# Interleaving two fp32 tensors: every tile DMA split into two, for the even and the odd partitions

## The chip, the core and the metric

The kernel runs on one core of a Trainium2 chip. The metric is the device time of one execution in microseconds (us); lower is better. Before the change the median of three runs was 314.24 us (314.24 to 314.25).

## What is computed

Two fp32 tensors of 32 x 256 x 1024 are interleaved element by element into one of twice the length. Nothing is calculated; every byte is read once, moved to its new place and written once.

```python
def reference(x, y):
    batch, seq, dim = x.shape          # 32, 256, 1024
    result = np.zeros((batch, seq, dim * 2), dtype=np.float32)
    result[..., 0::2] = x
    result[..., 1::2] = y
    return result
```

x and y are 33.55 MB each and the output is 67.11 MB, so 134.22 MB cross between HBM (the chip's large memory) and SBUF (the core's working memory, 128 partitions wide).

## The kernel before

Each tensor is taken as one flat run of elements and cut into n = 8 tiles of 128 x 8192 fp32 (4 MB). Partition p of a tile holds row p, a run of 8192 elements (32 KB) that lies in one piece in HBM. The output of one x tile and one y tile is 128 rows of 16384 elements; it is made and stored in two halves of 128 x 8192, called h = 0 and h = 1.

SBUF holds two tiles of x (`xt`), two of y (`yt`) and two output halves (`ot[0]` for h = 0, `ot[1]` for h = 1). Tile k uses `xt[k % 2]` and `yt[k % 2]`.

Three engines work, each with its own list of instructions, tied by semaphores:

- SyncE (SP) issues the loads. The first half of x's tile 0 is loaded at line 45, then y's tile 0 (line 55), and from there x's tile k (line 52) and y's tile k (line 55) in turn. From tile 2 on, SP waits before each load until VectorE has read the buffer for the last time: `woven` at 4(k-2)+3 for x (line 50) and 4(k-2)+4 for y (line 54).
- VectorE (DVE) does the interleaving with 32 copies of 128 x 4096 elements: for each half, line 67 writes the x elements to the even columns of `ot[h]` and line 70 the y elements to the odd ones. It waits for the loads (`xsem`, `ysem`, and `hsem` for the second half of x's tile 0) and for the stores of the same half of the tile before (`osem[h]`, line 66), whose buffer it overwrites. Each copy adds 1 to `woven`.
- ScalarE (ACT) issues the stores (line 76), one for each half as soon as both its copies are done; the very first half is stored in two parts, of 2048 and 6144 columns. It also loads the second half of x's tile 0 (line 46).

Each DMA adds 16 to its semaphore when it has ended, so the waits count in steps of 16; `stored(k, h)` at line 42 works out how many stores of half h came before tile k. In the profile, SP's DMAs run on queue q1 and ACT's on q10; both queues feed the same 16 DMA engines. After the kernel is built, `tile_interleave_kernel` moves the first DMA of SP and the first of ACT (lines 45 and 46) ahead of the program's opening barrier. At the end ACT and SP wait for the last stores and set the semaphores back.

In the order of the work only the semaphores matter: SP runs ahead up to two tiles, ACT follows VectorE, and VectorE needs a loaded tile and an output half whose last store has ended.

Of the kernel before, what the change touches and what calls it, by code (L numbers as in the profile page):

```python
# [3 lines left out]


def _interleave(nc, x, y, out):
    P = 128
    W = 8192
    H = W // 2  # L10

    total = 1
    for s in x.shape:
        total *= s
    n = total // (P * W)
    assert n * P * W == total

    def rows(ap, names, k):
        flat = ap.rearrange("b s d -> (b s d)")
        return flat[k * names : (k + 1) * names].rearrange("(p w) -> p w", p=P)  # L20

    fp32 = mybir.dt.float32
    xt = [nc.alloc_sbuf_tensor(f"xt{b}", [P, W], fp32).ap() for b in (0, 1)]
    yt = [nc.alloc_sbuf_tensor(f"yt{b}", [P, W], fp32).ap() for b in (0, 1)]
    ot = [nc.alloc_sbuf_tensor(f"ot{b}", [P, W], fp32).ap() for b in (0, 1)]

    xsem = [nc.alloc_semaphore(f"xsem{b}") for b in (0, 1)]
    hsem = nc.alloc_semaphore("hsem")
    ysem = [nc.alloc_semaphore(f"ysem{b}") for b in (0, 1)]
    woven = nc.alloc_semaphore("woven")  # L30
    osem = [nc.alloc_semaphore(f"osem{b}") for b in (0, 1)]

    xs = [rows(x, P * W, k) for k in range(n)]
    ys = [rows(y, P * W, k) for k in range(n)]
    os_ = [rows(out, 2 * P * W, k) for k in range(n)]

    Q = W // 4

    def parts(k, h):
        return [slice(0, W)] if k or h else [slice(0, Q), slice(Q, W)]  # L40

    def stored(k, h):
        return 16 * sum(len(parts(j, h)) for j in range(k))

    nc.sync.dma_start(out=xt[0][:, :H], in_=xs[0][:, :H]).then_inc(xsem[0], 16)
    nc.scalar.dma_start(out=xt[0][:, H:], in_=xs[0][:, H:]).then_inc(hsem, 16)
    for k in range(n):
        b = k % 2
        if k >= 2:
            nc.sync.wait_ge(woven, 4 * (k - 2) + 3)  # L50
        if k:
            nc.sync.dma_start(out=xt[b], in_=xs[k]).then_inc(xsem[b], 16)
        if k >= 2:
            nc.sync.wait_ge(woven, 4 * (k - 2) + 4)
        nc.sync.dma_start(out=yt[b], in_=ys[k]).then_inc(ysem[b], 16)

    for k in range(n):
        b = k % 2
        for h in (0, 1):
            c = slice(h * H, (h + 1) * H)  # L60
            if h == 0:
                nc.vector.wait_ge(xsem[b], 16 * (k // 2 + 1))
            elif k == 0:
                nc.vector.wait_ge(hsem, 16)
            if k:
                nc.vector.wait_ge(osem[h], stored(k, h))
            nc.vector.tensor_copy(out=ot[h][:, 0::2], in_=xt[b][:, c]).then_inc(woven, 1)  # L67
            if h == 0:
                nc.vector.wait_ge(ysem[b], 16 * (k // 2 + 1))
            nc.vector.tensor_copy(out=ot[h][:, 1::2], in_=yt[b][:, c]).then_inc(woven, 1)  # L70

    for k in range(n):
        for h in (0, 1):
            nc.scalar.wait_ge(woven, 4 * k + 2 * h + 2)
            for c in parts(k, h):
                nc.scalar.dma_start(
                    out=os_[k][:, h * W : (h + 1) * W][:, c], in_=ot[h][:, c]
                ).then_inc(osem[h], 16)

    nc.scalar.wait_ge(osem[0], stored(n, 0))  # L80
    used = sorted(s.num for s in [*xsem, hsem, *ysem, woven, osem[0]])
    assert used == list(range(used[0], used[-1] + 1)), used
    nc.scalar.sem_clear(range(used[0], used[-1] + 1))
    nc.sync.nop(nofuse=True).wait_op(osem[1], stored(n, 1), "sem-ge").then_inc(
        osem[1], -stored(n, 1)
    )


def kernel(tc, x, y, out):
    nc = tc.nc  # L90
    tc.close()
    tc.compile()

    _interleave(nc, x, y, out)

    blocks = nc.main_func.blocks
    for engine in (mybir.EngineType.SP, mybir.EngineType.Activation):
        opening = blocks[0].instructions
        at, moved = next(
            (b, i)  # L100
            for b in blocks[1:]
            for i in b.instructions
            if i.engine == engine and i.opcode == "DMACopy"
        )
        assert not (moved.sync_info and moved.sync_info.on_wait)
        body = at.instructions
        body.remove(moved)
        gate = next(
            n
            for n, i in enumerate(opening)  # L110
            if i.engine == engine and i.opcode == "Drain"
        )
        opening.insert(gate, moved)
        at.instructions = body
        blocks[0].instructions = opening


# [1 line left out]
_INS = ['x', 'y']  # L119
_OUTS = [((32, 256, 2048), 'float32')]  # L120


# [23 lines left out]
```

## Time and profile before

| | |
|---|---|
| median of 3 runs | 314.24 us |
| profiled execution | 314.21 us |
| its span, first to last instruction | 312.9 us |
| HBM read / written | 67.11 MB / 67.11 MB, 429 GB/s over the span |
| VectorE x copies, L67 | 16, mean 2295 ns |
| VectorE y copies, L70 | 16, mean 2288 ns |
| VectorE idle before L67 for a store to end | 206.3 us in 14 waits, longest 28.9 |
| a store of 4096 KB, issue to landing (median) | 34.1 us |
| a y load of 4096 KB, issue to landing (median) | 41.5 us |
| an x load of 4096 KB, issue to landing (median) | 24.4 us |

The span is what the profile covers; the execution has 1.3 us more around it. A DMA here is one instruction that moves a whole tile; the 16 DMA engines share its rows, and what the profile calls a packet is one row's transfer on one engine. "Share of 16 engines" is the summed time of the packets over sixteen times the span. The time from issue to landing of a DMA includes what it waits for behind others on the same engines. "L67" is line 67 of the kernel.

### The profile page before, as it was taken

Reading aid. Unit: us, or ns where it says so; the run is one execution under the profiler, and the core shown is the slowest. Engines: PE = TensorE matmul, PEld = TensorE weight load, DVE = VectorE, ACT = ScalarE, POOL = GpSimd, SP = SyncE. Lnnn points to the kernel's source line nnn. Section 1 sums busy time; section 2 is a strip of 40 time slices with the busy share of each in tenths; the row PEclk is TensorE's granted clock in tenths of the full one; section 3 lists DMA queues with packets and bytes.
Section 4 is the critical chain, followed back from the end, with each engine's and each line's share of the span. In section 5 each row is a group of like instructions: output and inputs, shape, how many; then the busy total and the mean of one; then the engine's idle time right before and its main releaser. Section 6 shows DMA issues by size and latency. Waiting matters only on the chain.

```text
span 312.9 us, 114 instructions
## 1 busy us (share of the span) xinstructions
DVE 71.9 (23%) x32; POOL 0.2 (0%) x4
## 2 busy tenths in 40 slices
DVE  0216000501305023050230503205032050415400
POOL 0000000000000000000000000000000000000000
DMA  8999999999999999999999999999999999999998
GB/s 344 461 406 431 436 402 431 440 465 406 448 423 431 440 406 465 402 469 402 469 402 465 406 457 415 436 436 419 452 402 469 402 469 402 469 402 461 411 444 360
DMA packets 4896, 134.22 MB, mean 429 GB/s; under 512 B 544, under 2 KB 544, under 8 KB 544
## 3 DMA queue, kind: packets, MB, share of 16 engines
q10 hardware_dynamic: 2592, 69.21, 51.3%
q1 hardware_dynamic: 2304, 65.01, 48.5%
HBM read 67.11 MB, written 67.11 MB: 429 GB/s over the span
## 4 chain that ended last, share of the span: by engine, by line
DMA 82%; DVE 12%; issue 0%
DMA out_dram<-ot 76%; DMA yt<-in_y_dram 7%; DVE ot L70 6%; DVE ot L67 6%
## 5 line engine op out<-in xcount | busy, mean ns | idle before, releaser
L67 DVE COPY ot<-xt 128x4096 f32<-128x4096 f32 x16 | 36.7, 2295 | 218.0 <-DMA out_dram<-ot 206.3
L70 DVE COPY ot<-yt 128x4096 f32<-128x4096 f32 x16 | 36.6, 2288 | 8.0 <-DMA yt<-in_y_dram 8.0
L130 POOL MEMSET const-uint8-127<- 128x1 uint8 x1 | 0.1, 102 | 0.0
L130 POOL MEMSET const-bfloat16-1.0<- 128x1 bf16 x1 | 0.1, 101 | 0.0
L130 POOL MEMSET const-float32-0.0<- 128x1 f32 x1 | 0.1, 98 | 0.2 <-issue 0.2
L130 POOL MEMSET const-float32-1.0<- 128x1 f32 x1 | 0.1, 98 | 0.0
## 6 DMA issues: line engine op xcount, KB each, us to landing
out_dram<-ot ACTq DMA_DIRECT2D x15, 4096.0 KB, 34.1
yt<-in_y_dram SPq DMA_DIRECT2D x8, 4096.0 KB, 41.5
xt<-in_x_dram SPq DMA_DIRECT2D x7, 4096.0 KB, 24.4
out_dram<-ot ACTq DMA_DIRECT2D x1, 3072.0 KB, 32.8
xt<-in_x_dram SPq DMA_DIRECT2D x1, 2048.0 KB, 11.7
xt<-in_x_dram ACTq DMA_DIRECT2D x1, 2048.0 KB, 13.4
out_dram<-ot ACTq DMA_DIRECT2D x1, 1024.0 KB, 16.1
```

Source lines behind the costliest of these rows:

```text
L67: nc.vector.tensor_copy(out=ot[h][:, 0::2], in_=xt[b][:, c]).then_inc(woven, 1)
L70: nc.vector.tensor_copy(out=ot[h][:, 1::2], in_=yt[b][:, c]).then_inc(woven, 1)
L130: nc = _bacc.Bacc("TRN2", target_bir_lowering=False, num_devices=1)
```

## The change

Partition 2i+r of a tile, with i from 0 to 63 and r 0 or 1, now holds row 64r+i in place of row 2i+r. As one DMA can't walk the partitions in that order, a helper `move` issues two: r = 0 moves rows 0 to 63 into or out of partitions 0, 2, ... 126, and r = 1 moves rows 64 to 127 into or out of partitions 1, 3, ... 127. Each adds 16 to the semaphore, so all counts of DMA semaphores double. All loads and stores go through `move`; x, y and the output halves are permuted alike, and VectorE's copies stay what they were. Two DMAs in place of one are moved ahead of the opening barrier on SP and on ACT.

```diff
+    R = 2
+
     def rows(ap, names, k):
+
         flat = ap.rearrange("b s d -> (b s d)")
-        return flat[k * names : (k + 1) * names].rearrange("(p w) -> p w", p=P)
+        return flat[k * names : (k + 1) * names].rearrange("(r i w) -> r i w", r=R, i=P // R)
+
+    def move(eng, sem, out, in_, c=slice(None), d=None):
+
+        d = c if d is None else d
+        for r in range(R):
+            to = out[r, :, d] if len(out.shape) == 3 else out[r::R, d]
+            of = in_[r, :, c] if len(in_.shape) == 3 else in_[r::R, c]
+            eng.dma_start(out=to, in_=of).then_inc(sem, 16)
...
     def stored(k, h):
-        return 16 * sum(len(parts(j, h)) for j in range(k))
+        return 16 * R * sum(len(parts(j, h)) for j in range(k))
 
-    nc.sync.dma_start(out=xt[0][:, :H], in_=xs[0][:, :H]).then_inc(xsem[0], 16)
-    nc.scalar.dma_start(out=xt[0][:, H:], in_=xs[0][:, H:]).then_inc(hsem, 16)
+    move(nc.sync, xsem[0], xt[0], xs[0], slice(0, H))
+    move(nc.scalar, hsem, xt[0], xs[0], slice(H, W))
...
-            nc.sync.dma_start(out=xt[b], in_=xs[k]).then_inc(xsem[b], 16)
+            move(nc.sync, xsem[b], xt[b], xs[k])
...
-        nc.sync.dma_start(out=yt[b], in_=ys[k]).then_inc(ysem[b], 16)
+        move(nc.sync, ysem[b], yt[b], ys[k])
...
-                nc.vector.wait_ge(xsem[b], 16 * (k // 2 + 1))
+                nc.vector.wait_ge(xsem[b], 16 * R * (k // 2 + 1))
...
-                nc.scalar.dma_start(
-                    out=os_[k][:, h * W : (h + 1) * W][:, c], in_=ot[h][:, c]
-                ).then_inc(osem[h], 16)
+                to = slice(h * W + c.start, h * W + c.stop)
+                move(nc.scalar, osem[h], os_[k], ot[h], c, to)
...
-    for engine in (mybir.EngineType.SP, mybir.EngineType.Activation):
+    for engine, count in ((mybir.EngineType.SP, 2), (mybir.EngineType.Activation, 2)):
+        for _ in range(count):
```

## The prediction, made before the changed kernel ran

> **What bounds the kernel now.** I read the page from its head: engines, then the DMA queues, then the chain, then the DMA issues.
>
> ```profile
> span 312.9 us, 114 instructions
> ## 1 busy us (share of the span) xinstructions
> DVE 71.9 (23%) x32; POOL 0.2 (0%) x4
> ...
> DMA packets 4896, 134.22 MB, mean 429 GB/s; under 512 B 544, under 2 KB 544, under 8 KB 544
> ## 3 DMA queue, kind: packets, MB, share of 16 engines
> q10 hardware_dynamic: 2592, 69.21, 51.3%
> q1 hardware_dynamic: 2304, 65.01, 48.5%
> ```
>
> The only computing engine works 23% of the time. The two DMA queues (q1 is SP's, q10 ACT's) together fill 51.3 + 48.5 = 99.8% of sixteen DMA engines. The packets count themselves: 34 DMAs of 128 rows are 4352, and 34 x 16 = 544 small ones carry the semaphore increments. So one row of a tile is one packet, each DMA gives each engine eight rows, and each engine ends its share with one small packet.
>
> ```profile
> DMA 82%; DVE 12%; issue 0%
> DMA out_dram<-ot 76%; DMA yt<-in_y_dram 7%; DVE ot L70 6%; DVE ot L67 6%
> ```
>
> The chain is DMA, with VectorE as its link. A chain step that is DVE is no idle time of the DMA engines: the busy time by stretches shows that they work through it.
>
> ```profile
> core 0: us, DVE busy (x) POOL busy (x), PEclk, DMA share, GB/s
> 0.00:12.00 12.00, 0.30 (x1) 0.20 (x4) 1.00 0.98 393
> 12.00:24.00 12.00, 3.98 (x2) 0.00 (x0) 1.00 1.00 431
> 24.00:58.00 34.00, 5.12 (x4) 0.00 (x0) 1.00 0.99 418
> 58.00:270.00 212.00, 49.06 (x22) 0.00 (x0) 1.00 1.01 434
> 270.00:303.00 33.00, 13.49 (x6) 0.00 (x0) 1.00 1.01 434
> 303.00:312.80 9.80, 0.00 (x0) 0.00 (x0) 1.00 0.87 374
> ```
>
> The reader is to see that the DMA share is full from 12 us to 303 us, whether loads alone run (431 GB/s at 12 to 24 us) or loads and stores (434). So the limit is one for each DMA engine, not for a direction. The trace's packet records give its size: 3777 of the 3840 packets of 32 KB took 1213 ns exactly, loads and stores alike. An engine's bytes, 134.22 MB / 16 / 32 KB = 256 such packets, need 256 x 1.213 = 310.5 us. That leaves 2.4 us of the span for the head (the first packet starts at 1.0 us, and the first 16 KB packets take 0.9 to 1.6 us each, later ones 0.61) and the tail. The profiled execution took 314.21 us, 1.3 more than its span; the median of the three runs is 314.24. What follows is counted from 314.21.
>
> One more thing lies in the packet records. The sixteen engines go in step: about 60.5 us all sixteen start a packet of q10 within 0.33 us, 1.21 us later all start one of q1, and the last round at 311 us still starts within 0.33 us. So at nearly every moment all engines move rows in one direction, and at the same place of their share.
>
> **The change, part by part.**
>
> Instructions. SP issues 32 DMAs for 16, ACT 36 for 18; VectorE's 32 copies are the same, on the same 128 partitions.
>
> ```profile
> 79.16 0.33 SPq L52 DMA_DIRECT2D xt<-in_x_dram  x1
> 81.36 0.33 SPq L55 DMA_DIRECT2D yt<-in_y_dram  x1
> ```
>
> An issue takes 0.33 us (0.33 to 0.48). The second x issue of a pair ends at about 79.8, and the next wait on SP opens at 81.36: 1.5 us of slack, nothing is late. On ACT the second store follows its first by about 0.34 us; the first gives each engine four rows, 4 x 1.213 = 4.9 us of work, so no engine runs dry. If an engine did, each of the 17 stores would cost up to 0.34 us, 5.8 us in all: that is the price without this cover, and I count 0. In the head the second x issue delays the opening barrier, and so y's first issue (1.57 us), by about 0.4 us; the first x tile gives the engines work until 11.7 us. Cost 0.
>
> Semaphore packets. Each engine gets 34 more, of 9 ns each (6 ns from start to the next packet's start): 0.2 to 0.3 us on the path that sets the end. No gap follows one today: the next packet starts at its end. I take 0.3. The waits on VectorE ask for twice the count and open when the second half has landed, which by bytes is the same moment: 0.
>
> Rows by engine. This is the part that decides. The bytes of one engine are unchanged if all sixteen take four rows of each half. But which rows lie side by side is new: a DMA now steps over every second partition. No row of the trace shows how 64 rows two partitions apart are dealt out, so I bound it. Lower end: a packet stays at 1213 ns and nothing is lost; 314.21 + 0.3 = 314.5. A gain has little room: the engines idle for some 1 us in all, at the head. Upper end: two engines stand on the same way into SBUF and take turns at the rate one of them has now, and each packet takes 2 x 1.213 = 2.426 us. Since the engines go in step, they would meet at every packet and not drift apart. What they save is their lag: while one is ahead, it has the way alone. The lag is 0 to 0.33 us, for two engines taken at random a third of that, 0.11, so 2.426 - 0.11 = 2.316 us a packet. 256 x 2.316 = 593 us, plus 2.4 of head and tail, 0.3 of semaphores and 1.3 outside the span: **597 us**. With a lag of 0 it is 625, with 0.33 it is 541.
>
> Which end? The nearest row is today's: sixteen engines in step, and none of the 32 KB packets after 43 us but one is longer than 1220 ns. If SBUF is reached through fixed groups of neighbouring partitions, today's dealing gives each engine a group of its own. There are three plain ways to deal 64 alternate rows four to an engine: four in a row (an engine's four rows now spread over eight neighbouring partitions); every sixteenth; or each row to the engine that has its partition today. In the first two, groups that one engine has to itself today are walked by two engines at the same time, while others stand idle; in the third nothing meets. Two of three, so I lean to the upper end, and keep both for the range.
>
> The Trainium skill says what such groups would be: "SBUF — State Buffer", section "Door 1: The DMA port swizzle", has sixteen ports, each for four partitions and the four that lie 32 higher, and gives a transfer of partitions 0 to 63 no more bandwidth than one of 0 to 31, about half of full. Judged by the partitions alone, its rule lets every half of this change reach all sixteen ports and would give 314.5 us; judged by what the engines reach at one moment, dealt four in a row, eight ports, and 597. No run here shows ports yet; that no packet of today is stretched agrees with one port for each engine.
>
> **The rivals.**
>
> *Not slower.* The dealing follows the partitions, or nothing is shared. Then only the 0.3 us of semaphores is left: 314.5, which is the same as before (0.2%, 0.63 us, is about what a measurement of this kernel can tell from no change). It decides at one point: whether a 32 KB packet keeps 1213 ns. For it speaks that every packet does so today, in both directions; against it, that this is the row of another dealing. The Trainium skill, "DMA: Bandwidth & Descriptors", section "Why a DMA increments its semaphore by 16 and not by 1", takes the number of engines from the row count alone, and 64 gives sixteen: by that each engine's bytes stay, which this rival and the forecast share.
>
> *One direction only.* Writes into SBUF meet and reads do not, or the reverse: 128 packets at 1.213 and 128 at 2.316 are 155 + 296 = 452, plus 4.0: 456 us.
>
> *Eight engines.* The change spreads a DMA over fewer engines than it says: eight engines would take 512 packets each, 621 + 4 = 625 us, with the DMA share at half and packets still 1213 ns. Against it: 128 rows go to all sixteen today, eight to each, and 64 divide as evenly.
>
> *A little slower.* The issue gap after each store shows after all (up to 5.8 us), or a memory effect stretches a few packets as at 27 to 42 us, where 59 were longer than 1220 ns, by about 0.15 us each: 315 to 321 us.
>
> *Faster.* Only the head could give more than 0.63 us, if the first 64 rows came sooner: 313.5.
>
> **How the numbers follow.** Meeting has two of three by the count of dealings: 0.56 for both directions (the forecast, 597, its own range 541 to 625) and 0.12 for one direction. Eight engines 0.06, a little slower 0.08, not slower 0.15, faster 0.03. Slower is the sum of the first four, 0.82; same 0.15; faster 0.03. The cases from 315 upward hold 0.82 only without their own tails, so the range takes in the not-slower case too: 314 to 626. It is wide because there are two answers far apart, and little between them.
>
> **What would show it.** The 32 KB rows' time shows in the page as queue share times span: 99.8% of 312.9 us now for 4352 rows. If the forecast holds, the DMA share stays near full while the mean falls from 429 GB/s to about 225, the packets rise to 5440 (1088 small ones), and stores take some 65 us from issue to landing instead of 34.1 for a whole tile. If engines are left out, the share falls to half. VectorE's copies stay at 2.29 us in every case. The prediction is wrong if the steady stretch still shows 434 GB/s: then the new dealing keeps the engines apart.

## The result, and the profile after

The changed kernel took 316.14 us (median of four runs, 315.43 to 316.48) beside 314.25 us for the kernel before: 1.0057 times, with a 95% interval of 1.0045 to 1.007. It is slower by 1.9 us, not by the 283 us of the forecast. The profiled execution took 316.48 us with a span of 315.1, so it stands 2.27 us above the profiled one of before.

The page after, engines, queues and chain:

```profile
span 315.1 us, 148 instructions
## 1 busy us (share of the span) xinstructions
DVE 72.0 (23%) x32; POOL 0.2 (0%) x4
...
DMA packets 5440, 134.22 MB, mean 426 GB/s; under 512 B 1088, under 2 KB 1088, under 8 KB 1088
## 3 DMA queue, kind: packets, MB, share of 16 engines
q10 hardware_dynamic: 2880, 69.21, 51.0%
q1 hardware_dynamic: 2560, 65.01, 48.3%
```

The packets are the foretold 4352 rows and 1088 semaphore packets, so all sixteen engines take part in each DMA. The queues' share times the span is (51.0 + 48.3)% of 315.1 = 312.9 us, for 312.3 before: the rows cost what they did. The stretches say the same (columns: span, VectorE's and GpSimd's busy time, clock, DMA share, GB/s):

```profile
0.00:12.00 12.00, 0.88 (x1) 0.20 (x4) 1.00 0.90 362
12.00:24.00 12.00, 2.75 (x2) 0.00 (x0) 1.00 1.02 441
...
58.00:270.00 212.00, 49.47 (x22) 0.00 (x0) 1.00 1.00 433
270.00:303.00 33.00, 13.49 (x6) 0.00 (x0) 1.00 0.99 429
303.00:315.00 12.00, 0.00 (x0) 0.00 (x0) 1.00 0.82 352
```

The long middle runs at 433 GB/s, as before at 434, and loads alone at 441 (12 to 24 us), for 431. In the packet records 3698 of the 3840 rows of 32 KB took 1213 ns, for 3777 before. So no engine waits for another at every packet, which is what the forecast rested on. The chain has the DMA and VectorE shares of before, and for the first time a per cent of issuing:

```profile
DMA 81%; DVE 12%; ACTq 1%; issue 0%; SPq 0%
DMA out_dram<-ot 75%; DVE ot L81 6%; DMA yt<-in_y_dram 6%; DVE ot L78 6%; ACTq L31 1%; SPq L31 0%
```

The loss shows at the two ends: in the first 12 us the DMA share is 0.90 for 0.98, and the last stretch is longer and emptier. The head in order of time, first before, then after (start, duration, queue, line, what, how many):

```profile
0.00 0.37 SPq L45 DMA_DIRECT2D xt<-in_x_dram  x1
0.12 0.37 ACTq L46 DMA_DIRECT2D xt<-in_x_dram  x1
...
1.57 0.33 SPq L55 DMA_DIRECT2D yt<-in_y_dram  x1
```

```profile
0.00 1.16 SPq L31 DMA_DIRECT2D xt<-in_x_dram  x2
0.12 1.31 ACTq L31 DMA_DIRECT2D xt<-in_x_dram  x2
...
2.75 1.11 SPq L31 DMA_DIRECT2D yt<-in_y_dram  x2
```

Two issues of 64 rows take 1.16 us where one of 128 took 0.37, and y's first load is issued at 2.75 us for 1.57. In the trace a 64-row issue by itself mostly takes 0.47 to 0.50 us, and a second right behind it 0.58 to 1.19 us, for 0.33 and 0.45 to 0.48 with 128 rows. The prediction had 0.33 for each. In the middle, where it showed two loads of 0.33 us each, the pairs now take 1.11 to 1.76 us; the longest are these:

```profile
81.11 1.66 SPq L31 DMA_DIRECT2D xt<-in_x_dram  x2
83.31 1.76 SPq L31 DMA_DIRECT2D yt<-in_y_dram  x2
```

The first pair ends at 82.77 us, and the second still starts 2.20 us after the first one's start, as before, when the copy that it waits for is done. So the longer issue is covered there.

The packet records give the sum. All figures are us for one engine, the mean of sixteen; "first engines done" is the idle time between an engine's last packet and that of the last engine.

| term | before | after | after, run again |
|---|---|---|---|
| idle up to 3 us (head) | 1.14 | 1.64 | 1.53 |
| packets longer than their usual time | 1.27 | 1.49 | 1.39 |
| packets at their usual time (1213 ns for 32 KB, 9 for a semaphore) | 310.97 | 311.28 | 311.28 |
| idle in the middle | 0 | 0.04 | 0 |
| first engines done | 0.19 | 1.51 | 0.25 |
| overlap of neighbouring packets | -1.08 | -1.18 | -1.18 |
| last packet ends | 312.50 | 314.78 | 313.25 |

The first profile of the changed kernel was an execution in which one engine fell behind. All others ended their last row at 312.95 to 313.56 us; this one still had a row to move then, and ended at 314.77. It lost its place in the middle of the run: followed back packet by packet, it was 0.4 us behind the median engine up to 150 us, and then four of its loads took 1.33, 1.45, 1.60 and 1.70 us in place of 1.21 (at 154.9, 164.7, 184.3 and 222.3 us), 1.23 us more in all. No other packet between 150 and 223 us took over 1.30 us. Another execution (the last column, 315.07 us) has no such engine and ends 1.5 us earlier. So there are four terms: 0.31 for semaphores (0.2 net of overlap), 0.4 to 0.5 for a later and more ragged start, 0.1 to 0.2 for packets longer than usual, and up to 1.3 for an engine that falls behind, which differs from run to run.

### The profile page after: what moved, and what is told of

The parts are those of the page before. It is cut to its first block, busy times and chain, and to the rows that moved or that the text cites. A ratio compares the mean times of both kernels' runs of the same rounds, so it can differ in the third digit from the quotient of the medians.

```text
span 315.1 us, 148 instructions
## 1 busy us (share of the span) xinstructions
DVE 72.0 (23%) x32; POOL 0.2 (0%) x4
## 2 busy tenths in 40 slices
DMA packets 5440, 134.22 MB, mean 426 GB/s; under 512 B 1088, under 2 KB 1088, under 8 KB 1088
## 3 DMA queue, kind: packets, MB, share of 16 engines
q1 hardware_dynamic: 2560, 65.01, 48.3%
## 4 chain that ended last, share of the span: by engine, by line
DMA 81%; DVE 12%; ACTq 1%; issue 0%; SPq 0%
DMA out_dram<-ot 75%; DVE ot L81 6%; DMA yt<-in_y_dram 6%; DVE ot L78 6%; ACTq L31 1%; SPq L31 0%
```

## The experiments

The first two questions were why no rows met, and where the 1.9 us are. The kernels below are edits of the changed kernel, or of the first one where it says so.

**Halves in place of alternate partitions.**

```diff
-            to = out[r, :, d] if len(out.shape) == 3 else out[r::R, d]
-            of = in_[r, :, c] if len(in_.shape) == 3 else in_[r::R, c]
+            to = out[r, :, d] if len(out.shape) == 3 else out[r * 64 : r * 64 + 64, d]
+            of = in_[r, :, c] if len(in_.shape) == 3 else in_[r * 64 : r * 64 + 64, c]
```

> Two DMAs of 64 rows for each tile transfer as in the changed kernel, but partition 64r+i holds row 64r+i: the DMAs take partitions 0 to 63 and 64 to 127. Same number of DMAs, rows, bytes and semaphore packets as the changed kernel. Theory 'ways': the engines reach SBUF by ways that belong to fixed groups of partitions, and the changed kernel escaped only because its even and odd partitions are dealt so that no two engines share one. Then half of the partitions at a time leaves half of the ways, 32 KB packets go from 1.213 us to about 2.3 us, and the time to about 540 to 625 us, as worked out in the prediction. Rival 'no ways': it does not matter which partitions a DMA touches, packets stay at 1.213 us and the time is that of the changed kernel, 315.4 to 316.5 us.

Measured: 471.87 us median of four runs (394.43, 468.2, 475.55 and 476.51). The stretches are those of the 475.55 us execution; the one of 394.43 us left no trace, so what made it shorter isn't shown:

```profile
12.00:24.00 12.00, 2.29 (x1) 0.00 (x0) 1.00 1.02 224
24.00:58.00 34.00, 6.70 (x3) 0.00 (x0) 1.00 1.01 221
58.00:270.00 212.00, 31.48 (x14) 0.00 (x0) 1.00 1.00 300
```

The DMA engines are as full as ever (1.00), and move half: 224 GB/s where loads run alone, for 431 before. A 32 KB packet mostly takes 2.38 us there. The rows of HBM that each DMA takes, and their order, are those of the changed kernel; only the partitions differ. So the ways into SBUF that the prediction supposed exist, and two engines on one share it as its upper end had it. It is not 2.3 us throughout, though: between 120 and 270 us loads took 2.03 and stores 1.44 us on average, 1.73 together. The records show what goes with it: 75% of that time 7 to 10 of the sixteen engines load while the others store, where in the first kernel all load or all store together for 76% of the time. This fits engines that meet, drift until one loads and its partner stores, and then hinder each other less; that reads and writes have a way each is what it suggests. The records don't name the partners, and no run measures it alone.

**Eight DMAs of 16 rows.** `R = 2` becomes `R = 8`, and the counts of DMAs ahead of the barrier 2 become 8.

> R = 8: partition 8i+r holds row 16r+i, and each tile transfer becomes eight DMAs of 16 rows, one row for each engine, over every eighth partition. Theory 'ways': if a way serves neighbouring partitions in groups of four and the ones 32 higher (the table of the page on SBUF in the Trainium skill), sixteen partitions eight apart stand on only half of the ways, however they are dealt, so packets take about 2.3 us and the kernel 540 to 630 us. Rival 'no ways': packets stay at 1.213 us, each engine gets 238 more semaphore packets of 9 ns than the first kernel, 2.1 us, and with more issue work at the head the time is 317 to 326 us.

Measured: 468.44 us (one run).

```profile
12.00:24.00 12.00, 1.24 (x1) 0.00 (x0) 1.00 1.07 221
58.00:270.00 212.00, 31.48 (x14) 0.00 (x0) 1.00 1.00 305
```

The same two rates as with halves, though these partitions are spread over the whole of SBUF. It is not how far the partitions spread that counts, but which. The Trainium skill, "SBUF — State Buffer", section "Door 1: The DMA port swizzle", puts partitions 0 to 63 on half of the sixteen ports, and by its table sixteen partitions eight apart stand on half of them too; both runs agree, with 224 and 221 GB/s for 431.

**Four DMAs of 32 rows.** `R = 4`, and 4 for the counts ahead of the barrier.

> R = 4: partition 4i+r holds row 32r+i, four DMAs of 32 rows, two rows for each engine, over every fourth partition. The runs with halves and eighths showed that engines meet where a DMA's partitions lie on few ways; the changed kernel's alternate partitions did not. Theory 'dealt to its own way': the dealing follows the row's number in such a manner that each engine keeps one way of its own also at a step of four (engine c of the lower eight takes partitions 4c+r and 32 higher): packets stay at 1.213 us, and the time is that of the changed kernel plus 68 more semaphore packets of 9 ns, 0.6 us, and a longer head, 316 to 319 us. Theory 'four in a row': neighbouring rows go to one engine, here two rows eight partitions apart at most, and engines four apart in number stand on one way: packets of 1.4 to 2 us as in halves, 390 to 480 us.

Measured: 316.46 us median of four runs, 1.0064 (1.0051 to 1.0078).

```profile
58.00:270.00 212.00, 49.47 (x22) 0.00 (x0) 1.00 1.01 433
```

No packet is stretched by a neighbour: the 32 KB packets take 1213 ns on average between 120 and 270 us. If neighbouring rows went to one engine ("four in a row" with 64, two in a row with 32), pairs of engines would stand on one way here and in the changed kernel, eight pairs of engines that are together whenever the two are at the same place of their share. They don't, and they have not slid apart either: ten of the sixteen engines start here within 0.28 us (2.06 to 2.34 us), so at least two pairs are in step, and up to 12 us each of their 16 KB rows takes 0.61 to 0.68 us. A dealing that fits this run and the changed kernel is the one which 128 rows would have, taken by the row's number: two halves of eight engines, and within a half two groups of neighbouring rows for each engine. Alternate partitions then put each engine's four rows on the partitions that it has today. The records don't name engine and partition, so this dealing is inferred from what meets and what doesn't. Halves do not bear it out: with the groups that the expectation for eighths names, it would put four engines on one way at a time, and the 2.38 us for 1.21 are those of two. How 64 rows in one block are dealt stays open.

**Tile 0 undivided, all others split**, and **tile 0 alone split.** A function gives the number of parts for each tile:

```diff
-    R = 2
+    def Rk(k):
+        return 2 if k else 1        # the other run: 1 if k else 2
...
-        return 16 * R * sum(len(parts(j, h)) for j in range(k))
+        return 16 * sum(Rk(j) * len(parts(j, h)) for j in range(k))
```

> The changed kernel with tile 0 left undivided (R = 1: its loads and stores are the DMAs of 128 rows of the first kernel); tiles 1 to 7 are split into even and odd partitions. Theory 'head': the 1.9 us that the change cost come from the head (first packet at 1.31 us for 1.00, engines started 1 us apart for 0.45 us, one engine a packet behind at the end) because a 64-row DMA takes longer to issue; without it only the semaphore packets are left, 314.4 to 314.9 us. Rival 'each DMA': the extra DMAs cost alike wherever they stand, 1.9 us / 34 = 0.056 us each; 29 of the 34 extra ones are left here (tile 0 has five transfers of its own: x in two parts, y, and the stores, of which h = 0 is in two), so about 315.7 to 315.9 us.

Measured: 314.58 us, 1.0011 (1.0002 to 1.0019). (28 of the extra DMAs are left, not 29: tile 0 has six transfers.)

> The other way about: only tile 0 is split into even and odd partitions, tiles 1 to 7 are whole. Theory 'head': nearly the whole loss is here, 315.4 to 316.3 us. Rival 'each DMA': six extra DMAs at 0.056 us, 314.5 to 314.6 us.

Measured: 316.87 us (314.59 to 317.61, eight runs), 1.0068 (1.0045 to 1.0091).

With seven of eight tiles split the kernel loses 0.36 us of 1.9; with one of eight split it loses 2.6, more than the whole change. A price for each DMA is out. The page with tile 0 undivided against that of tile 0 split, line by line:

```profile
span 313.4 us, 142 instructions
...
DMA packets 5344, 134.22 MB, mean 428 GB/s; under 512 B 992, under 2 KB 992, under 8 KB 992
```

```profile
span 316.3 us, 120 instructions
...
DMA packets 4992, 134.22 MB, mean 424 GB/s; under 512 B 640, under 2 KB 640, under 8 KB 640
```

More semaphore packets and less time: 992 - 544 = 448 more of 9 ns are 28 for each engine, 0.25 us, and they are most of the 0.36. In the second kernel twelve engines had ended by 313.0 us, and the other four ended at 314.3, 314.6, 315.1 and 315.9; again the end is set by the last one, and this time it is 2.9 us late.

**Which part of tile 0?** Four edits of the first kernel. In `first_columns` each of tile 0's transfers is two DMAs of 128 rows and half the columns; in `first_loads` and `first_stores` its loads or its stores alone are two DMAs, over even and odd partitions; `first_both` does both. In these the rows keep their places (row p in partition p):

```diff
+    def move(eng, sem, out, in_, c):
+        for r in (0, 1):
+            eng.dma_start(out=out[r::2, c], in_=in_[r::2, c]).then_inc(sem, 16)
...
-                nc.scalar.dma_start(
-                    out=os_[k][:, h * W : (h + 1) * W][:, c], in_=ot[h][:, c]
-                ).then_inc(osem[h], 16)
+                to = os_[k][:, h * W : (h + 1) * W]
+                if k:
+                    nc.scalar.dma_start(out=to[:, c], in_=ot[h][:, c]).then_inc(osem[h], 16)
+                else:
+                    move(nc.scalar, osem[h], to, ot[h], c)
```

> The first kernel with tile 0 alone divided, but by columns: each of its six transfers is two DMAs of 128 rows of half the length. As many DMAs at the head as in the run that splits tile 0 alone into even and odd partitions (316.87 us). Theory 'slow issue of 64 rows': 128-row DMAs issue in 0.33 to 0.37 us, so the engines start less far apart and no engine falls behind by a packet: 314.2 to 314.8 us. Rival 'two DMAs ahead of the barrier': the second DMA on SP and on ACT is what spoils the head whatever its shape, 315.5 to 317.5 us.

Measured: 314.41 us median of eleven runs, but three of them at 315.37, 315.50 and 316.59; 1.0017 (1.0003 to 1.0031).

> The first kernel (row p in partition p) with the loads of tile 0 alone issued as two DMAs each, even and odd partitions; stores and all else whole. Theory 'engines start apart': the lag is made where the first loads start, so most of the loss of the run with tile 0 split is here: 315.5 to 317.5 us. Rival 'stores': the loss comes from the six store DMAs that ACT issues in a row at 24.7 to 30.2 us: 314.3 to 314.7 us here.

Measured: 314.52 us, all eleven runs between 314.42 and 314.59; 1.0008 (0.9999 to 1.0016).

> The counterpart: the stores of tile 0 alone as two DMAs each, even and odd partitions; all loads whole. Theory 'engines start apart': 314.3 to 314.7 us. Rival 'stores': 315.5 to 317.5 us.

Measured: 314.32 us, all eleven between 314.23 and 314.54; 1.0003 (0.9994 to 1.0012).

> The first kernel with both the loads and the stores of tile 0 as two DMAs each over even and odd partitions, but with row p still in partition p, so each DMA takes every second row of HBM. It joins the two edits that cost 0.25 and 0.05 us by themselves. It differs from the run that lost 2.65 us by the order of the rows in HBM alone. Theory 'rows in HBM': the loss needs the new order of the rows (64r+i in partition 2i+r), so 314.4 to 314.8 us here. Rival 'together': split loads and split stores of one tile together let an engine fall behind, whatever the order of the rows: 315.5 to 317.6 us.

Measured: 314.64 us median of twelve, eleven of them between 314.54 and 314.72 and one at 316.82; 1.0015 (1.0003 to 1.0027).

Both theories on loads and stores fell: neither makes the loss by itself. `first_loads` has the whole ragged head (the first packet at 1.32 us for 1.00, y's first load issued at 2.76 us) and costs 0.25 us. So the start by itself is worth 0.25. `first_both` came out where theory 'rows in HBM' had it, but for one execution. An engine that falls behind is another matter: a late start does not make it certain, and with 128-row DMAs in `first_columns` three of eleven runs are late without the longer issue. The profile of `first_both` caught its one late execution. Followed back from its last packet, each packet starting as the one before it on the same engine ends, the records of the engine that ended last read, in ns (start, duration, bytes, queue):

```
37940  309  8192 q10
38245 1213 32768 q1
39455  309  8192 q10
39761 1213 32768 q1
40970  309  8192 q10
41276 2766 32768 q1
44038    9     4 q10
```

One row loaded at 41.28 us took 2.77 us for 1.21. Other engines' loads at that moment took about 1.55. The engine is 1.1 us behind the median one from there on, and nothing brings it back: each engine moves its own 8.39 MB, and none takes over another's rows. That load is only half of its delay. Two more long rows follow, 1.73 us at 87.6 us and 1.89 us at 95.4 us, and it ends at 315.1 us, 2.1 us after the thirteen engines that stay together (by 313.0 us). Two others fall behind as well, without such a load at 41 us: many rows of 1.25 to 1.73 us from 88 us on bring them to 314.2 and 314.3 us. In the tile-0-split run it is much the same for the engine that ended last: 2.53 us at 41.37 us, then 1.73 us at 88.1 and 2.17 us at 94.7 us. Such a cluster of longer loads near 40 to 42 us is in the first kernel too, 14 packets of 1226 to 1395 ns. There, in the execution that was profiled, no engine is struck much harder than the others, and they stay together.

**The order of the rows in HBM.** The changed kernel with partition 2i+r holding row 2i+r again; each DMA takes every second row of HBM:

```diff
-        return flat[k * names : (k + 1) * names].rearrange("(r i w) -> r i w", r=R, i=P // R)
+        return flat[k * names : (k + 1) * names].rearrange("(i r w) -> r i w", r=R, i=P // R)
```

> The changed kernel with one letter pair exchanged in the view of HBM: partition 2i+r holds row 2i+r again, so the two DMAs of a transfer, still over even and odd partitions, take the even and the odd rows. All tiles are split, 68 DMAs, the same issues, semaphores and partitions as in the changed kernel. Theory 'rows in HBM': 314.5 to 315.0 us, the semaphore packets and 0.3 us at the head are left. Rival 'together': 315.4 to 316.9 us, as the changed kernel.

> The changed kernel itself, beside the two runs above on the same chip, to see how its times spread: 315.4 to 316.9 us, and if an engine falling behind by a packet is a matter of chance, here and there one at about 314.7.

Measured: 315.16 us for the exchanged order (314.92 to 316.38, nine runs), 1.0032 (1.0022 to 1.0043); 315.85 us for the changed kernel beside it (315.07 to 316.28, six runs), 1.0047 (1.0034 to 1.006). The exchanged order lies between the two forecasts, and the intervals overlap, so this does not settle whether the order of rows has a part. With tile 0 alone split, the old order was late in one run of twelve and the new one in six of eight, which speaks for a part, though the two ran on different chips. The first kernel itself, beside the last runs, took 315.17 us in one execution of twenty, and at most 314.55 in the others: a late one is rare there, but not unknown. The best run of the changed kernel, 315.07, is the one profiled in the last column of the table above: 0.8 us over the first kernel without any engine behind.

## Why the prediction was wrong

- *The rows by engine.* This is the step that failed. The prediction counted three plain ways to deal 64 rows, found that engines meet in two, and put 0.68 on meeting. Its picture of ways was right (halves and eighths show them), and so was its upper price where engines load alone (2.38 us for a foretold 2.316, or 2.426 without a lag). But at steps of two and four partitions no two engines meet: 1213 ns a packet and 433 GB/s, as the third kind of dealing would have it. Counting ways of dealing as equal was no evidence, and no row of the trace before could tell them apart; it took a run with fewer rows. That 316.14 us lies between 314 and 626 is no merit, as the range was drawn around both answers.
- *The price if they had met.* 2.316 us for each packet rested on engines that stay in step. With halves the middle of the run gave 1.73 us on average, and 394 to 477 us for the kernel where 541 to 625 had been worked out: the size was off even for the case it was meant for.
- *The rival that came true* is "not slower" in its mechanism (1213 ns to the packet, 433 GB/s in the middle) and "a little slower" in its range (315 to 321). Of the two reasons given for the latter, the issue gap after the stores doesn't show (0 to 0.04 us idle in the middle). Stretched packets do: 105 rows of 32 KB took over 1220 ns, for 60 before, and four of them made the late engine of the first profile. The prediction gave this case 0.08.
- *Issues.* Counted at 0.33 us each, they take 0.47 to 1.19. In the middle this is covered as was said: the share stays at 1.00. In the head it was costed at 0 because the first x tile gives the engines work until 11.7 us. That holds for y's delayed load, but not for the first packets, which start 0.3 us later and less together: 0.25 us with the loads of tile 0 alone, 0.4 to 0.5 in the profiles.
- *Semaphore packets.* 0.2 to 0.3 foretold; 0.31 by the records, 0.2 net; with tile 0 undivided 0.36 in all.
- *What was not thought of.* The prediction took the engines' common step as given for the whole run. An engine that loses its place keeps its delay to the end, and the end waits for the last one: 1.2 us in the first profile here (314.77 for 313.56), 2.9 with tile 0 alone split.
- *Waits, VectorE and the number of engines* were as foretold: copies at 2.29 us, 1088 small packets.

What stays open: what stretches single rows, around 41 us and again from 88 us on, and why it strikes one engine more than the others in most runs of the split tile 0 with the new row order, in few with the old one, and in none with loads or stores split alone.

## What to carry to other kernels

Where DMA engines are full, ask of a new access pattern not how many partitions or engines it has but whether, row by row, two engines stand on the same way into SBUF: half the partitions in one block halved the rate of loads here (224 GB/s for 431), alternate ones cost nothing in the middle (433 for 434). A sum over sixteen engines ends with the slowest one; compare the mean of the engines with the last, at the end of the run. And splitting a DMA costs least in the middle and most at the head: 28 extra DMAs behind tile 0 cost 0.36 us, six in tile 0 cost 0.39 us with the old order of rows and 2.65 with the new one. Of this, the later start with tile 0's loads split, whose longer issue nothing covers there, accounts for 0.25 us.

## What the hardware showed that was not expected

- A DMA of 64 rows takes longer to issue than one of 128: 0.47 us for 0.33, with blocks of partitions (0.47) as with alternate ones, with 32 rows 0.47 to 0.48 and with 16 rows 0.49 to 0.50.
- Engines that share a way do not stay in step: most of the time 7 to 10 of 16 load while the others store (75% of the time with halves, 67% with eighths), and the rate rises from 224 to 300 GB/s and from 221 to 305.
- Where no two engines meet, they need no common step: between 120 and 270 us all sixteen moved rows in one direction 13% of the time with four DMAs of 32 rows, for 76% in the first kernel, and 22% and 70% in the two profiles of the changed one. The middle runs at 433 to 434 GB/s in each of them.
